# The last output unit of a two-layer decoder trunk: where its residual is added, how its blocks are multiplied, which queue stores

## Chip, cores, metric

One Trainium2 chip, one of its cores. The metric is the device time of one execution in microseconds (us), as the median of several runs. Engines: TensorE (PE, its weight loads PEld), VectorE (DVE), ScalarE (ACT), GpSimd (POOL), SyncE (SP). VectorE, ScalarE and TensorE work on SBUF and on PSUM, where the matmuls accumulate.

## What is computed

Two layers on x of 256 tokens by 2048 features in float32. Layer 0 is forgetting attention (32 heads of 64, logits with a cumulated forget gate), layer 1 is sliding-window attention with sinks and partial rotary. Each has a SiLU gate path, an output projection and a residual; a final RMSNorm closes:

```python
for i in range(DEPTH):
    h = rmsnorm(x, norm_g[i])
    p = h @ w_in                      # q, k, v, gate
    y = attention(q, k, v) * silu(gate)
    x = x + y @ w_out                 # residual
return rmsnorm(x, final_g)
```

The change lies in the last two of these lines of the second layer, for the last 256 of the 2048 features.

## The kernel before

The activations lie with features on partitions: `xT` is 128 partitions x 16 k-tiles x 256 tokens. A float32 product is made of rounded parts: weights and activations are split into a high and a low part (ScalarE casts the high part, line 220, VectorE subtracts for the low one, line 221), and high x high, high x low and low x high are accumulated. The weights come in units of 256 columns. Each has four parts of four k-tiles, which SyncE loads into four raw buffers (line 207); split weights lie in five buffers.

A unit has two blocks, c = 0 and 1 (`block(unit, p, c)`, for part p). Most units (`halves`) multiply wide and narrow: per k-tile one matmul of 512 columns, whose moving operand is the high and the low part side by side, and later one of 256. The high-high and the cross products then lie in two halves of a PSUM bank and are added by VectorE when the unit is consumed. The last unit, `last_out[7]` (`halves=False`, `apart`), has tokens on partitions instead: block c is token half c, it has an accumulator of its own, and the plain branch makes three matmuls of 256 columns per k-tile into one half bank. Accumulators rotate over the two buffers of pool `ps_acc`; a new one waits until the reader of the one before last is done.

The order on TensorE is that of the program text (`keep_in_program_order`). On the other engines a planner orders by priority and readiness. Steps are counted by `tick()`, four for a part's block, so 32 for a unit; `after(n, fn)` issues `fn` n steps later, with raised priority.

The tail. Units 0 to 6 of the last projection add their residual in `xT` on VectorE (lines 697 and 698), square (line 712, summed on GpSimd, line 718) and scale by the norm's weights. `tail_residual`, 20 steps after layer 1's norm, turns the last two k-tiles of `xT` by four TensorE transposes into `tail_x` (tokens on partitions). `columns`, 16 steps after unit 6, makes the sum of squares of units 0 to 6 per token. In the last unit all four parts of c = 0 come first, then those of c = 1. When a block is done, `finish(th, ps)` adds `tail_x` (line 782), sums squares (line 786), makes r = 1/sqrt by Ln and Exp and one Newton step (lines 789 to 797) and multiplies by the last weights (line 798). `scale` then spreads r over partitions by a matmul (`rows`), multiplies the other 14 k-tiles by it in four pieces (`scaled`, line 811) and stores all. For th = 0 `scale` comes `SCALE_DUE` = 8 steps later, that is after two parts of c = 1; for th = 1 at once. Stores alternate between SyncE's and ScalarE's queues.

Of the kernel before, what the change touches and what calls it, by code (L numbers as in the profile page):

```python
# [10 lines left out]
F32 = mybir.dt.float32  # L11
F32R = mybir.dt.float32r
AF = mybir.ActivationFunctionType
ALU = mybir.AluOpType
AX = mybir.AxisListType

P = 128
S = 256
D = 2048
KT = D // P  # L20
# [37 lines left out]
def trunk(  # L58
# [19 lines left out]
    def mm(*args, **kw):  # L78
        tc.keep_in_program_order(nc.tensor.matmul(*args, **kw))  # L79

    def transpose(out, in_, ident):
        tc.keep_in_program_order(nc.tensor.transpose(out, in_, ident))  # L82
# [22 lines left out]
    def after(steps, fn):  # L105
        due.setdefault(clock[0] + max(steps, 1), []).append(fn)
# [117 lines left out]
    def block(unit, p, c):  # L224
        _, _, _, kt0, s = unit.parts[p]
        w, a = loaded[unit, p], unit.acts
        if p == 0 and (c == 0 or unit.apart):

            pool, tag, banks = unit.apart if c == 1 else (*unit.acc, 2)
            ps = pool.tile([P, banks, 512], F32, tag=tag, name="acc")  # L230
            if unit.apart:
                unit.ps[c] = ps[:, 0, :]
            else:
                unit.ps, unit.both = [ps[:, i, :] for i in range(2)], ps
        n = unit.n if unit.kind == "tok" else S
        both, ps = unit.ps[c], unit.ps[c][:, 0:n]
        cs = slice(c * P, (c + 1) * P)
        def operands(i):

            kt = kt0 + i  # L240
            if unit.kind == "tok":
                return a[:, kt, 0, cs], a[:, kt, 1, cs], w[:, i]
            return w[:, i, 0, cs], w[:, i, 1, cs], a[:, kt]

        first, last = kt0 == 0, kt0 + s == KT
        ops = [operands(i) for i in range(s)]
        def done():
            if p < len(unit.parts) - 1:
                return
            if unit.apart:  # L250
                unit.consume(c, both)
            elif c == 1 and unit.kind == "tok":
                for i in range(2):
                    unit.consume(i, unit.ps[i])
            elif c == 1:
                unit.consume(unit.both)

        def narrow():
            for i, (_, sl, mv) in enumerate(ops):
                mm(ps, sl, mv[:, 0, :], start=False, stop=last and i == s - 1)  # L260
                if i % 2:
                    tick()
            done()

        if unit.halves:

            for i, (sh, _, mv) in enumerate(ops):
                mm(both, sh, mv.rearrange("p h n -> p (h n)"), start=first and i == 0, stop=False)
                if i % 2:
                    tick()  # L270
            if s % 2:
                tick()
            return narrow
        if n == 512:
            for i, (sh, sl, mv) in enumerate(ops):
                mm(ps, sh, mv[:, 0, :], start=first and i == 0, stop=False)
                mm(ps, sh, mv[:, 1, :], start=False, stop=False)
                tick()
                mm(ps, sl, mv[:, 0, :], start=False, stop=last and i == s - 1)
                tick()  # L280
        else:
            for i, (sh, sl, mv) in enumerate(ops):
                mm(ps, sh, mv[:, 0, :], start=first and i == 0, stop=False)
                mm(ps, sl, mv[:, 0, :], start=False, stop=False)
            for i, (sh, _, mv) in enumerate(ops):
                mm(ps, sh, mv[:, 1, :], start=False, stop=last and i == s - 1)
                tick()
        done()
        return lambda: None
# [434 lines left out]
    def to_layer1(m):  # L724
        split_x(m, 1)
        square_into(sums1, m)
        if m == KT - 1:

            def norm():
                nonlocal swa  # L730
                fox_scope.__exit__(None, None, None)
                swa = ctx.enter_context(tc.tile_pool(name="swa", bufs=2))
                state["r1"] = r = inv_rms(
                    sums1, "n1", ps_s.tile([P, 2, 512], F32, tag="S", name="ps_n1")[:, 0, :]
                )
                rope = swa.tile([P, 2, S], F32, name="rope_c", bufs=1)
                nc.sync.dma_start(out=rope, in_=rope_d)
                nc.vector.tensor_mul(rope, rope, r[:, 0:S].unsqueeze(1).to_broadcast([P, 2, S]))
                state["rr"] = rope
                after(20, tail_residual)  # L740

            after(19, norm)

# [2 lines left out]
    FM = KT - 2  # L746
    tail = {}

    def tail_residual():
        pt = ps_t.tile([P, 512], F32, tag="T", name="pt_r")  # L750
        for th in range(2):
            for j in range(2):
                o = (2 * th + j) * P
                transpose(pt[:, o : o + P], xT[:, FM + j, th * P : (th + 1) * P], ident)
        tail["x"] = swa.tile([P, 2, 2 * P], F32, name="tail_x", bufs=1)
        nc.scalar.copy(tail["x"], pt.rearrange("p (t f) -> p t f", t=2))

    def to_end(m):
        square_into(sums2, m)
# [18 lines left out]

    def finish(th, ps):
        t = slice(th * P, (th + 1) * P)  # L780
        x = tail["x"][:, th, :]
        nc.vector.tensor_add(x, ps[:, 0 : 2 * P], x)
        rest = work.tile([P, 2, 3 * P], F32, tag="st", name="rest").rearrange("p a b -> p (a b)")
        xg, sq = rest[:, 0:S], rest[:, S : 2 * S]
        ss, v, r, w = (work.tile([P, 1], F32, tag=f"tail{i}", name=f"tail{i}") for i in range(4))
        nc.vector.tensor_tensor_reduce(
            out=sq, in0=x, in1=x, scale=1.0, scalar=0.0, op0=ALU.mult, op1=ALU.add, accum_out=ss
        )
        nc.vector.tensor_scalar(
            v, ss, 1.0 / D, tail["ss"][:, th : th + 1], op0=ALU.mult, op1=ALU.add  # L790
        )
        nc.scalar.activation(r, ss, AF.Ln, scale=1.0 / D, bias=tail["ss"][:, th : th + 1])
        nc.scalar.activation(r, r, AF.Exp, scale=-0.5)

        nc.vector.scalar_tensor_tensor(out=w, in0=r, scalar=-0.5, in1=r, op0=ALU.mult, op1=ALU.mult)
        nc.vector.tensor_scalar(w, w, v, 1.5, op0=ALU.mult, op1=ALU.add)
        nc.vector.tensor_mul(r, r, w)
        nc.vector.tensor_mul(xg, x, tail["g"])

        def scale():  # L800
            rows = ps_s.tile([P, 2, 512], F32, tag="S", name="rows")[:, 0, :]
            mm(rows[:, 0:P], r.to_broadcast([P, P]), ident, start=True, stop=True)
            nc.scalar.mul(xg, xg, r)
            nc.scalar.dma_start(out=tail_d[th], in_=xg)

            scaled = wpool.tile([P, 2048], F32, tag="w", name="scaled")
            scaled = scaled[:, 0 : FM * P].rearrange("p (m t) -> p m t", t=P)
            m0 = 0
            for i, n in enumerate((2, 4, 4, 4)):
                m1 = m0 + n  # L810
                nc.vector.tensor_mul(  # L811
                    scaled[:, m0:m1, :], xT[:, m0:m1, t],
                    rows[:, 0:P].unsqueeze(1).to_broadcast([P, n, P]),
                )
                eng = (nc.sync, nc.scalar)[i % 2]
                eng.dma_start(out=out_d[th, :, m0:m1, :], in_=scaled[:, m0:m1, :])
                m0 = m1

        if th == 0:
            after(SCALE_DUE, scale)  # L820
        else:
            scale()
# [195 lines left out]
    for i, (u, p) in enumerate(stream):  # L1018
        if u in paired:
            if p % 2 == 0:  # L1020
                if prev is not None:
                    block(*prev, 1)()
                    prev = None
                fetch(i + WBUFS)
            held += [block(u, p, c) for c in range(2)]
            if p % 2:
                for k, narrow in enumerate(held):
                    narrow()
                    if k == 1:
                        fetch(i + WBUFS)  # L1030
                held = []
            continue
        fetch(i + 1 + LOOK)
        if u is last_out[7]:
            if p == 0 and prev is not None:
                block(*prev, 1)()
            block(u, p, 0)()
            continue
        block(u, p, 0)()
        if prev is not None:  # L1040
            block(*prev, 1)()
        prev = (u, p)
    for p in range(len(last_out[7].parts)):
        block(last_out[7], p, 1)()


# [63 lines left out]
```

## Time and profile before

| | us |
|---|---|
| median of 3 runs (lowest, highest) | 823.14 (822.63, 824.35) |
| the profiled execution | 824.22 |
| its span, first to last instruction | 822.5 |
| TensorE busy | 812.5 |
| VectorE busy | 633.2 |
| ScalarE busy | 526.5 |
| GpSimd busy | 57.8 |

The span is what the profiler saw between the first and the last instruction; the time of the execution is a little longer. The mean granted TensorE clock was 0.997 of full speed. In the rows below, a timeline row is start, length, engine, line, operation, output and inputs, and how many instructions it merges; in brackets stands how long the engine had been idle before it and what ended that. A row of weight loads (LDWEIGHTS) shows at what moment TensorE takes up each matmul.

### The profile page before, as it was taken

To read this page: it belongs to the slowest core of one execution; us is meant where nothing else is said; L and a number is where in the kernel's file an instruction comes from. 1 tells how busy PE (TensorE), PEld (TensorE's weight loads), DVE (VectorE), ACT (ScalarE), POOL (GpSimd) and SP (SyncE) were. 2 spreads that over 40 slices of the span, in tenths; PEclk is the share of its full clock that TensorE was granted. 3 is DMA by queue.
4 is the path that set the end of the run, shared out by engine and by line. 5 is a ranking of instruction groups with operands and counts; after the bars stand their busy time and mean duration, and the time that the engine had idled before them with its cause. 6 is when DMAs were issued, how large, how long until landed. Compare 5 with 4: busy or idle time off the path is not lost.

```text
span 822.5 us, 13113 instructions
## 1 busy us (share of the span) xinstructions
PE 812.5 (99%) x4738; PEld 707.4 (86%) x4738; DVE 633.2 (77%) x1179; ACT 526.5 (64%) x978; POOL 57.8 (7%) x96
## 2 busy tenths in 40 slices
PE   9999999999999999999999999999999999999996
PEld 8888888888888888888888888888888888887886
DVE  6998866887668776788749668788999899976655
ACT  6875765675666665575737555577678776875642
POOL 1012010100001010020002110000000000001210
PEclk9999999999999999999999999999999999999998
DMA  8766665665656565565555555655455454464642
GB/s 286 234 219 228 192 205 181 192 201 174 190 188 182 190 212 179 181 196 160 178 186 183 191 191 162 200 179 176 130 174 174 156 166 152 154 194 145 205 128 103
DMA packets 47264, 150.49 MB, mean 183 GB/s; under 512 B 5552, under 2 KB 7248, under 8 KB 47200
## 3 DMA queue, kind: packets, MB, share of 16 engines
q1 hardware_dynamic: 44640, 141.71, 54.1%
q0 software_dynamic: 1408, 6.36, 2.8%
q10 hardware_dynamic: 1152, 1.60, 0.5%
q8 instruction: 37, 0.61, 0.3%
q14 instruction: 27, 0.22, 0.1%
HBM read 147.50 MB, written 2.15 MB: 182 GB/s over the span
## 4 chain that ended last, share of the span: by engine, by line
PE 96%; DMA 2%; DVE 1%; SPq 1%; ACT 0%; issue 0%; DVEq 0%; ACTq 0%
PE acc L79 88%; PE ps_s L79 3%; PE psy L79 3%; PE pt L82 1%; DMA wraw<-in_vf_dram 1%; PE pt_w L82 1%; DMA wraw<-in_fox_in_dram 1%; SPq L207 0%; DVE xs L155 0%; DVE scaled L811 0%; DVE w L221 0%; PE ps_n L79 0%; SPq L930 0%; DVE ssq L942 0%; PE rows L79 0%
## 5 line engine op out<-in xcount | busy, mean ns | idle before, releaser
L79 PE MATMUL acc<-xs,w 128*128 128x512 f32 (+1 forms) x2624 | 478.1, 339 | 0.4 <-ACT w L220 0.4
L79 PEld LDWEIGHTS acc<-xs,w 128*128 128x128 f32 x2624 | 405.1, 190 | 54.4 <-issue 1.3
L221 DVE TENSOR_TENSOR w<-wraw,w 128x1024 fp32r<-128x1024 f32 (+4 forms) x277 | 324.7, 1181 | 115.5 <-ACT w L220 113.5
L220 ACT CAST w<-wraw 128x1024 fp32r<-128x1024 f32 (+4 forms) x277 | 276.7, 1009 | 135.6 <-PE acc L79 99.9
L79 PE MATMUL acc<-ys,w 128*128 128x512 f32 (+1 forms) x960 | 169.7, 338 | 0.0
L79 PEld LDWEIGHTS acc<-ys,w 128*128 128x128 f32 x960 | 147.5, 189 | 20.5 <-issue 0.6
L79 PE MATMUL acc<-w,xs 128*128 128x512 f32 (+2 forms) x512 | 110.8, 364 | 0.5 <-ACT w L220 0.5
L79 PEld LDWEIGHTS acc<-w,xs 128*128 128x128 f32 x512 | 86.9, 191 | 14.6 <-ACT w L220 0.8
L335 ACT ACTIVATE st<-st,mx 128x128 f32<-128x128 f32 (+1 forms) x128 | 56.6, 445 | 17.1 <-DVE mx L639 17.1
L293 ACT COPY half<-acc 128x512 f32<-128x512 f32 x56 | 32.8, 585 | 9.5 <-PE acc L79 8.8
L79 PE MATMUL ps_s<-kk,q 128*128 128x256 f32 (+1 forms) x160 | 31.2, 309 | 0.1
L718 POOL TENSOR_TENSOR acc<-acc,sq 128x256 f32<-128x256 f32 x28 | 23.7, 848 | 89.0 <-ACT sq L712 87.9
L390 DVE CUSTOM_DVE_ANT_0 st<-ps_s,st 128x128 f32<-128x128 f32 (+1 forms) x96 | 28.1, 330 | 0.4
L79 PEld LDWEIGHTS ps_s<-kk,q 128*128 128x128 f32 x160 | 24.3, 189 | 3.2 <-issue 0.8
L517 ACT CAST ys<-gt 128x512 fp32r<-128x512 f32 x16 | 9.9, 619 | 22.8 <-DVE gt L516 22.8
L424 ACT COPY pts<-pt 128x384 f32<-128x384 f32 x32 | 15.2, 474 | 14.4 <-PE pt L82 14.1
L335 ACT ACTIVATION_READ_ACCUMULATOR st<-st,mx 128x1 f32 x128 | 24.1, 188 | 0.0
L716 POOL COPY acc<-sq 128x256 f32<-128x256 f32 x2 | 1.3, 674 | 323.5 <-ACT sq L712 323.5
L626 POOL DMA_DIRECT2D bc<-negc_d x16 | 8.8, 552 | 216.8 <-DVE st L415 144.0
L310 ACT ACTIVATE gate_e<-gt 128x512 f32<-128x512 f32 x16 | 10.1, 628 | 21.3 <-DVE gt L323 21.3
L123 POOL TENSOR_SCALAR_AFFINE_SELECT bc<-bc 128x256 f32<-128x256 f32 x32 | 18.7, 605 | 71.0 <-DMA bc<-negc_d 71.0
L154 ACT ACTIVATE xs<-xT,g_sb 128x256 fp32r<-128x256 f32 x32 | 15.5, 501 | 12.8 <-DVE xT L698 12.0
(144 smaller groups left out, 596.9 us busy)
## 6 DMA issues: line engine op xcount, KB each, us to landing
wraw<-in_fox_in_dram SPq DMA_DIRECT2D x96, 512.0 KB, 4.5
wraw<-in_swa_in_dram SPq DMA_DIRECT2D x72, 512.0 KB, 3.9
wraw<-in_fox_out_dram SPq DMA_DIRECT2D x32, 512.0 KB, 3.9
wraw<-in_swa_out_dram SPq DMA_DIRECT2D x32, 512.0 KB, 4.1
wraw<-in_fox_in_dram SPq DMA_DIRECT2D x54, 256.0 KB, 4.2
bc<-negc_d POOLq DMA_DIRECT2D x16, 384.0 KB, 5.3
wraw<-in_vf_dram SPq DMA_DIRECT2D x4, 288.0 KB, 5.2
xT<-in_xt_dram SPq DMA_DIRECT2D x2, 512.0 KB, 9.2
```

The costliest lines, as they stand in the source:

```text
L79: tc.keep_in_program_order(nc.tensor.matmul(*args, **kw))
L82: tc.keep_in_program_order(nc.tensor.transpose(out, in_, ident))
L123: return nc.gpsimd.affine_select(out=ap, in_=ap, compare_op=ALU.is_ge, fill=NEG, base=base, pattern=pattern, channel_multiplier=mult,)
L154: nc.scalar.activation(xs[:, kt, 0, :], xT[:, kt, :], AF.Copy, scale=g)
L220: state["split"] = nc.scalar.copy(high, raw)
L221: nc.vector.tensor_tensor(out=low, in0=raw, in1=high.bitcast(F32), op=ALU.subtract)
L293: nc.scalar.copy(s, ps[:, :, S : 2 * S])
L310: nc.scalar.activation(e, z, AF.Abs)
L335: nc.scalar.activation(st[:, hh, rng], st[:, hh, rng], AF.Exp, bias=nm[:, qb, hh : hh + 1], accum_out=l[:, qb, hh : hh + 1],)
L390: nc.vector.tensor_tensor_reduce(out=st, in0=high, in1=st, scale=self.scale, scalar=LOWEST, op0=ALU.add, op1=ALU.max, accum_out=self.mx[:, ...
L424: nc.scalar.copy(group.new_pts(self.j, hh)[:, hh, self.j, :], pt[:, 0 : 3 * P])
L718: nc.gpsimd.tensor_add(sums[0], sums[0], s)
```

## The change

Four edits, all for the last unit.

1. `tail_residual` no longer uses TensorE, PSUM and ScalarE. VectorE turns `xT`'s last two k-tiles in blocks of 32 x 32, one GpSimd DMA writes the result to a DRAM tile, and 16 GpSimd DMAs (128 rows of 32 elements each) read it back in the right order into `tail_x`. It is timed 150 steps after the step that was followed by 20.
2. Block c = 0 of the last unit takes the wide and narrow branch. Its `finish` adds both halves of the bank, so it has one VectorE add more.
3. The first part of block c = 1 moves up to just behind the second part of c = 0. Then VectorE adds the residual of th = 1 to that accumulator in PSUM, and the other three parts accumulate on top, after c = 0 is done. `finish(1)` reads PSUM directly: no add, and the squares are summed by ScalarE instead of VectorE.
4. All stores of th = 0 go through SyncE's queue; those of th = 1 still alternate.

```diff
-        if unit.halves:
+        if unit.halves or (unit.apart and unit.kind == "tok" and unit.n == 256 and c == 0):
...
         else:
+            seeds = bool(unit.apart) and n == 256
+            kw = {"skip_group_check": True} if seeds else {}
...
-                mm(ps, sh, mv[:, 1, :], start=False, stop=last and i == s - 1)
+                mm(ps, sh, mv[:, 1, :], start=False, stop=(last or seeds) and i == s - 1, **kw)
...
-                after(20, tail_residual)
+                after(150, tail_residual)
...
+    turned_d = dram.tile([P, 2, 4, 64], F32, name="turned_d")
+
     def tail_residual():
-        pt = ps_t.tile([P, 512], F32, tag="T", name="pt_r")
-        for th in range(2):
-            for j in range(2):
-                o = (2 * th + j) * P
-                transpose(pt[:, o : o + P], xT[:, FM + j, th * P : (th + 1) * P], ident)
-        tail["x"] = swa.tile([P, 2, 2 * P], F32, name="tail_x", bufs=1)
-        nc.scalar.copy(tail["x"], pt.rearrange("p (t f) -> p t f", t=2))
+        turned = swa.tile([P, 2, 4, 64], F32, name="turned", bufs=1)
+        nc.vector.transpose(
+            turned.rearrange("p t b (k j) -> p k (t b) j", k=2),
+            xT[:, FM:KT, :].rearrange("p k (b j) -> p k b j", j=32),
+        )
+        nc.gpsimd.dma_start(out=turned_d, in_=turned)
+        x = tail["x"] = swa.tile([P, 2, 2 * P], F32, name="tail_x", bufs=1)
+        rows = turned_d.rearrange("(a i) t b (k j) -> a t b i k j", a=4, k=2)
+        cols = x.rearrange("p t (k a j) -> a t p k j", k=2, a=4)
+        for t in range(2):
+            for a in range(4):
+                for k in range(2):
+                    nc.gpsimd.dma_start(out=cols[a, t, :, k], in_=rows[a, t, :, :, k])
...
     def finish(th, ps):
-        x = tail["x"][:, th, :]
-        nc.vector.tensor_add(x, ps[:, 0 : 2 * P], x)
+        if th == 0:
+            x = tail["x"][:, th, :]
+            nc.vector.tensor_add(x, ps[:, 0:S], x)
+            nc.vector.tensor_add(x, ps[:, S : 2 * S], x)
+        else:
+            x = ps[:, 0:S]
...
-        nc.vector.tensor_tensor_reduce(
-            out=sq, in0=x, in1=x, scale=1.0, scalar=0.0, op0=ALU.mult, op1=ALU.add, accum_out=ss
-        )
+        if th == 0:
+            nc.vector.tensor_tensor_reduce(
+                out=sq, in0=x, in1=x, scale=1.0, scalar=0.0, op0=ALU.mult, op1=ALU.add, accum_out=ss
+            )
+        else:
+            nc.scalar.activation(sq, x, AF.Square, accum_out=ss)
...
-            nc.scalar.dma_start(out=tail_d[th], in_=xg)
+            (nc.sync, nc.scalar)[th].dma_start(out=tail_d[th], in_=xg)
...
-                eng = (nc.sync, nc.scalar)[i % 2]
+                eng = (nc.sync, nc.scalar)[i % 2 * th]
...
             block(u, p, 0)()
+            if p == 1:
+                block(u, 0, 1)()
+                seeded = u.ps[1][:, 0:S]
+                nc.vector.tensor_add(seeded, seeded, tail["x"][:, 1, :])
             continue
...
-    for p in range(len(last_out[7].parts)):
+    for p in range(1, len(last_out[7].parts)):
         block(last_out[7], p, 1)()
```

More of the change, by code (lines that the diff above doesn't have):

```diff
@@ L281, in block @@
         else:
+            seeds = bool(unit.apart) and n == 256
+            kw = {"skip_group_check": True} if seeds else {}
             for i, (sh, sl, mv) in enumerate(ops):
-                mm(ps, sh, mv[:, 0, :], start=first and i == 0, stop=False)
-                mm(ps, sl, mv[:, 0, :], start=False, stop=False)
+                mm(ps, sh, mv[:, 0, :], start=first and i == 0, stop=False, **kw)
+                mm(ps, sl, mv[:, 0, :], start=False, stop=False, **kw)
             for i, (sh, _, mv) in enumerate(ops):
-                mm(ps, sh, mv[:, 1, :], start=False, stop=last and i == s - 1)
+                mm(ps, sh, mv[:, 1, :], start=False, stop=(last or seeds) and i == s - 1, **kw)
                 tick()
```

## The prediction

> **What bounds the kernel now.** I read the page's busy rows first, then the whole chain of waits with TensorE's own waits, and last the timeline of the final 20 us, where most of the change sits.
>
> ```profile
> PE 812.5 (99%) x4738; PEld 707.4 (86%) x4738; DVE 633.2 (77%) x1179; ACT 526.5 (64%) x978; POOL 57.8 (7%) x96
> ...
> PE 96%; DMA 2%; DVE 1%; SPq 1%; ACT 0%; issue 0%; DVEq 0%; ACTq 0%
> ...
> PE rows L79 <- DVE tail L797: 2.3, 1, 2.3
> ```
>
> TensorE is busy for 99% of the span, carries 96% of the chain, and the longest it ever waits for another engine is 2.3 us, once, in the last unit's tail (the columns of a wait: us in all, times, longest). So time comes off in two ways only: less work on TensorE anywhere, or a shorter stretch behind its last matmul. That stretch, from the chain that ended last:
>
> ```profile
> 814.32 0.43 DVE tail_x L782
> ...
> 814.78 0.42 DVE rest L786
> ...
> 815.25 0.30 ACT tail L792
> ...
> 815.81 0.17 DVE tail L795
> ...
> 816.25 0.17 DVE tail L797
> ...
> 816.56 0.47 PE rows L79 x2
> ...
> 818.07 1.20 DVE scaled L811 x2
> ```
>
> I call E the moment the add L782 starts (814.32). From E the root r is ready after 2.10 us (816.42), its three small steps beginning at E+1.49 (815.81); rows and scaled end at 819.27, and the span ends 3.2 us later, when the stores have landed. The profiled execution took 824.22 us around a span of 822.5; the median of the runs is 823.14, 1.08 lower. I sum against 824.22 and move the difference onto the median.
>
> **The change part by part.** *The transposes off TensorE.* Here are the weight-load rows around the four removed transposes, and those around like groups of four (start, length of the group, instructions). A ScalarE copy goes with them; TensorE doesn't wait for it, so it counts as 0.
>
> ```profile
> 506.32 0.59 PEld L82 LDWEIGHTS pt_r<-ident,xT 128*128 128x128 f32 x4
> 506.87 6.10 PEld L79 LDWEIGHTS acc<-w,xs 128*128 128x128 f32 x35
> ...
> 549.70 0.46 PEld L82 LDWEIGHTS pt_w<-ident,st 128*128 128x128 f32 x4
> 550.13 5.64 PEld L79 LDWEIGHTS acc<-xs,w 128*128 128x128 f32 x32
> 555.71 0.46 PEld L82 LDWEIGHTS pt_w<-ident,st 128*128 128x128 f32 x4
> ```
>
> From the first load to the next unit's load the four took 0.55 us; the like group took 0.43 (549.70 to 550.13). TensorE has no slack there, so all of it comes off: 0.43, between 0.35 (an estimate: 0.43 less the spread of 0.1 between these two) and 0.55.
>
> In its place VectorE turns 512 elements per partition. That form isn't in the trace; the nearest row is the shuffle of the same shape. GpSimd gets 17 DMA issues. In the rows of two stretches of 12 us below, the columns behind the stretch's length are PE, PEld, DVE, ACT and POOL busy.
>
> ```profile
> L838 DVE STREAM_SHUFFLE rot<-rot_t 128x512 f32<-128x512 f32 x9 | 6.7, 743 | 0.0
> ...
> 534.00:546.00 12.00, 12.00 (x75) 10.76 (x74) 8.77 (x22) 7.00 (x17) 0.00 (x0) 1.00 0.55 176
> 546.00:558.00 12.00, 12.00 (x74) 10.70 (x73) 11.93 (x30) 11.01 (x28) 0.00 (x0) 1.00 0.57 175
> ...
> L737 SPq DMA_DIRECT2D rope_c<-in_rope_dram x1: 328/328/328, 419.4 to 419.4; - x1
> ...
> L626 POOL DMA_DIRECT2D bc<-negc_d x16 | 8.8, 552 | 216.8 <-DVE st L415 144.0 <-DVE mx L390 46.6 <-issue 22.0
> ```
>
> 150 steps are 130 later than now. A unit is 32 steps, so 506.4 moves four units on, to about 554, where VectorE is busy 11.93 of 12 us. If the 0.74 us stands ahead of the fold that pt_w at 555.71 reads, TensorE could wait up to 0.74. I take 0: only TensorE keeps program order, and an operation without a late input is moved forward freely (rope's load, written in the same norm step as the residual's timer, went out at 419.4), so the idle 3 us in 534 to 546 are as likely a place. GpSimd's 17 issues are 17 x 0.55 = 9.4 us on an engine at 0.00 there; nobody reads tail_x before about 806. Zero, but see the second rival.
>
> *First block wide and narrow.* Per k-tile three 256-column matmuls become one of 512 and one of 256. The rows of the last unit:
>
> ```profile
> 801.83 5.83 PEld L79 LDWEIGHTS acc<-w,ys 128*128 128x128 f32 x48
> ...
> 804.21 0.69 DVE L698 TENSOR_TENSOR xT<-acc,xT 128x512 f32<-128x512 f32 x1
> ...
> 805.49 1.55 POOL L718 TENSOR_TENSOR acc<-acc,sq 128x256 f32<-128x256 f32 x2 [8.65 <-ACT sq L712]
> ...
> 807.59 0.54 PEld L79 LDWEIGHTS ps_cols<-ones,acc 128*128 128x128 f32 x4
> 807.91 0.42 DVE L782 TENSOR_TENSOR tail_x<-acc,tail_x 128x256 f32<-128x256 f32 x1 [3.02 <-PE acc L79]
> ...
> 808.05 2.94 PEld L79 LDWEIGHTS acc<-w,ys 128*128 128x128 f32 x24
> ...
> 809.85 0.16 DVE L797 TENSOR_TENSOR tail<-tail,tail 128x1 f32<-128x1 f32 x1
> ...
> 810.91 0.31 PEld L79 LDWEIGHTS rows<-ident,tail 128*128 128x128 f32 x2
> 811.14 2.94 PEld L79 LDWEIGHTS acc<-w,ys 128*128 128x128 f32 x24
> 811.45 2.21 DVE L811 TENSOR_TENSOR scaled<-xT,rows 128x256 f32<-128x256 f32 x4 [1.44 <-PE rows L79]
> ```
>
> 48 in 5.76 us and 24 in 2.86 make 0.1197 us each, 0.359 per k-tile. A wide and a narrow one cost (555.71 - 550.13)/16 = 0.349. Sixteen k-tiles: -0.17. Not under zero gain, since the columns are the same; at most 0.33 (0.020 a k-tile, if the second block's pace is the slower 2.94/24). The second add for th = 0 has a price on VectorE, below.
>
> *A new wait.* The second block's first part now comes after two parts of the first. There are two accumulators: the first block takes one, the second must take unit 6's, which VectorE gives back when L698 ends, at 804.90. Two parts of 4 x 0.349 bring TensorE to 801.83 + 2.79 = 804.62, its matmul to 804.74 (0.12 behind the load); with 0.14 from VectorE's end to TensorE's start (816.42 to 816.56) it starts at 805.04. So +0.30, in a place where TensorE doesn't wait today (the block began at 808.05); from 0 to 0.4. Everything on TensorE queues behind it. The seed add waits for those 12 matmuls and has nothing behind it on VectorE until the columns.
>
> From there: second block part 0 (1.44) to 806.36, part 2 (1.40) to 807.75, columns (0.46) to 808.21, whose sum GpSimd has at 807.04, part 3 to 809.61, then 24 matmuls (2.87) to 812.48 for rows. Is r of th = 0 there? Add at 809.61 + 0.32, then 2.10 as today (807.91 to 810.01) and 0.46 for the second add: 812.49, load 0.11 later at 812.60. So +0.12 (0 to 0.25): the cover of 0.9 us that r had today is used up by the added VectorE step and the faster first block. Rows 0.23, last 12 matmuls 1.44, to 814.27, where today it is 814.01: E moves +0.26 (-0.17 + 0.30 + 0.12, rounded), without the transposes.
>
> *The end of th = 1.* The add goes (the residual is in PSUM) and the square goes to ScalarE. Its price, from an activation with a sum:
>
> ```profile
> 545.05 0.49 ACT L335 ACTIVATE st<-st,mx 128x256 f32<-128x256 f32 x1
> 545.46 0.19 ACT L335 ACTIVATION_READ_ACCUMULATOR st<-st,mx 128x1 f32 x1
> ...
> L473 ACT COPY pts<-pt_w x16: 350/362/380, 550.5 to 737.8; 128x256 f32<-128x256 f32 x16
> L475 DVE TENSOR_TENSOR pts<-pt_w,apart x16: 658/684/692, 551.3 to 738.2; 128x512 f32<-128x512 f32 x16
> ```
>
> 0.60 us, then 0.56 through Ln and Exp (815.25 to 815.81): the small steps could begin at E+1.18 instead of E+1.49. But VectorE isn't free: rows of th = 0 used to have 24 matmuls behind them, now 12. Its four scaled products run from 812.60 + 0.54 to 815.35, which is E+0.77 with E at 814.58. Then the product with tail_g (0.34) and v (0.20): E+1.31. I take -0.18, at best -0.31.
>
> *Stores.* Five of th = 0 on SyncE at 0.34 each; its last leaves near 815.7. ScalarE's queue is free for the Square. Cost 0 to 0.2, if they still drain when th = 1's begin near 817.5; I take 0, from their 2.1 us to landing:
>
> ```profile
> out_dram<-scaled SPq DMA_DIRECT2D x2, 256.0 KB, 2.1
> ```
>
> Sum: -0.43 - 0.17 + 0.30 + 0.12 - 0.18 = -0.36 us: 823.9 against 824.22, and 822.8 against the median. All ends together: -0.55 - 0.33 + 0 + 0 - 0.31 = -1.2, and -0.35 + 0 + 0.4 + 0.25 + 0.1 + 0.2 + 0.74 = +1.3 (the 0.1 if the tail loses slightly, the 0.74 the turn).
>
> **The rivals.** *The product first.* L473 and L475 read one PSUM tile from two engines; the last copy starts at 737.8, takes 0.36, and the product starts at 738.2: not together. If the product with tail_g is put ahead of the Square, it runs from E+0.77 to E+1.19, the Square after it, and the small steps begin at E+2.37, 0.88 later than today: sum +0.70, 823.8. The code writes the Square first, which speaks against it. The Trainium skill ("PSUM — Partial Sum Buffer", section "PSUM bank collisions raise a hardware error") says that two engines may not touch one bank in the same partitions at once, reads included; the trace agrees in the two rows named. Were it not so, the two could overlap and their order would cost nothing.
>
> *Slower: the gather holds up weights.* 16 transfers of 128 rows of 128 bytes pass the same 16 DMA engines as the weights.
>
> ```profile
> q0 software_dynamic: 1408, 6.36, 2.8%
> ...
> q10 hardware_dynamic: 1152, 1.60, 0.5%
> ...
> wraw<-in_swa_in_dram SPq DMA_DIRECT2D x72, 512.0 KB, 3.9
> ...
> 553.85 0.33 SPq L207 DMA_DIRECT2D wraw<-in_swa_in_dram  x1
> ...
> 562.50 1.05 ACT L220 CAST w<-wraw 128x1024 fp32r<-128x1024 f32 x1
> ```
>
> q10's packet costs 0.5% x 822.5 x 16 / 1152 = 57 ns, q0's 262 ns (they are larger). 128 packets an engine are 7.3 to 34 us. With four raw buffers, the load issued at 553.85 is cast four casts on, at 562.50: 8.65 us less 3.9 to land leaves 4.75. Loads sharing the engines half and half take 7.8: hidden. It decides once a load is held over 4.75 us: all 7.3 us ahead of one load would cost 2.5, sum +2.2: 825.3. GpSimd's pace of 0.55 us an issue speaks against such a heap. The Trainium skill's page "DMA: Bandwidth & Descriptors" (section "Measured") calls transfers under 64 KB descriptor-dominated, 0.68 us at 4 KB and 0.95 at 64; sixteen of 16 KB would be, as an estimate, 11 to 15 us on end, which no run here shows yet.
>
> *Everything fits:* no accumulator wait, no wait for r, the best prices: 821.9.
>
> **How the numbers follow.** The sum as forecast 0.62; the product first 0.1; slower by the gather 0.08; everything fits 0.2. Two tenths of a per cent are 1.65 us, about what a measurement of this kernel can tell from no change. Forecast and product-first lie within it, a wait behind the turn too; the everything-fits case is 0.4 us short of the bound at 821.5, and the runs scatter by more than that (822.63 to 824.35), so I let 0.12 of its 0.2 pass it. Faster 0.12, within 0.80, slower 0.08. Predicted 822.8, range 821.4 to 824.3: the low end is everything-fits with 0.5 of spread, the high end the sum's upper end (824.4).
>
> **What would show it.** The pt_r rows gone from TensorE; one TensorE wait on L698 of 0.2 to 0.4 us near 804.6; E between 814.0 and 814.3; rows of th = 0 within 0.2 us of r; the Square at E, its small steps at E+1.3 behind scaled; no new ScalarE waits on wraw while GpSimd issues. A wait of TensorE anywhere in 500 to 600, or stores that still land more than 3.4 us after the last scaled product, would make it wrong.

## The result, and the profile after

| us | before | after |
|---|---|---|
| median of 8 runs (lowest, highest) | 823.22 (822.63, 824.35) | 825.34 (824.97, 827.04) |
| the profiled execution, its span | 824.22, 822.5 | 825.25, 823.5 |
| layer 1's first weight load (U) to the last unit's first load | 310.20 | 311.20 |
| from there to the end of the last scaled product | 17.44 | 17.51 |
| from there to the end of the span | 3.23 | 4.04 |

The ratio of the times is 1.0025, with an interval of 1.0016 to 1.0034: the change costs 2.1 us, and the forecast had the wrong sign. What lies ahead of U varies from one execution to the next (U is 491.63 in the profile before, 490.75 after, and the code ahead of it is the same), so the three stages are counted from U; they add up to +1.88. The end of the span is shown to a tenth of a us, so the third stage is good to 0.05 us, and a difference of two such to 0.1. Stages of equal code agree well: the first was 310.20, 310.21 and 310.21 in the three kernels in which nothing ahead of the last unit differs. Only the last unit, which I had worked out most closely, came out as forecast.

The rows of the page and of its waits that answer to those of before:

```profile
span 823.5 us, 13100 instructions
...
PE 812.2 (99%) x4718; PEld 706.8 (86%) x4718; DVE 634.4 (77%) x1179; ACT 526.3 (64%) x979; POOL 67.9 (8%) x113
...
PEld ps_n L79 <- POOL acc L720: 1.6, 1, 1.6
PE rows L79 <- DVE tail L815: 2.1, 1, 2.1
```

TensorE has 20 instructions fewer and is busy 0.3 us less, GpSimd 10 us more. The wait of the tail has shrunk from 2.3 to 2.1, and a wait that was not there before has come: TensorE on GpSimd, 1.6 us, in layer 1's norm (`ps_n` is the matmul that spreads the sum of squares). This is the place, by the timeline of before and then of after:

```profile
491.63 6.80 PEld L79 LDWEIGHTS acc<-xs,w 128*128 128x128 f32 x38
496.56 1.62 POOL L718 TENSOR_TENSOR acc<-acc,sq 128x256 f32<-128x256 f32 x2 [9.52 <-ACT sq L712]
498.17 2.36 DVE L221 TENSOR_TENSOR w<-wraw,w 128x1024 fp32r<-128x1024 f32 x2 [0.59 <-ACT w L220]
498.48 0.42 PEld L79 LDWEIGHTS ps_n<-acc,ones 128*128 128x128 f32 x2
```

```profile
490.75 6.80 PEld L79 LDWEIGHTS acc<-xs,w 128*128 128x128 f32 x38
494.78 0.71 DVE L756 STREAM_TRANSPOSE turned<-xT 128x512 f32<-128x512 f32 x1
496.05 0.57 POOL L760 DMA_DIRECT2D turned_d<-turned  x1 [9.89 <-DVE xs L155]
496.64 0.76 POOL L720 TENSOR_TENSOR acc<-acc,sq 128x256 f32<-128x256 f32 x1
497.28 1.22 DVE L221 TENSOR_TENSOR w<-wraw,w 128x1024 fp32r<-128x1024 f32 x1 [0.77 <-ACT w L220]
497.48 1.61 POOL L720 TENSOR_TENSOR acc<-acc,sq 128x256 f32<-128x256 f32 x1
498.43 1.74 DVE L221 TENSOR_TENSOR w<-wraw,w 128x1024 fp32r<-128x1024 f32 x1
499.14 0.30 PEld L79 LDWEIGHTS ps_n<-acc,ones 128*128 128x128 f32 x2 [1.59 <-POOL acc L720]
500.07 5.41 POOL L767 DMA_DIRECT2D tail_x<-turned_d  x8 [0.98 <-DMA turned_d<-turned]
```

Read it from U. The turn is written for a moment 150 steps after the norm, but it went out at U+4.03, *inside* the norm, and its write to DRAM was put ahead of the last two sums of squares in GpSimd's queue. Before, the sums began at U+4.93 and ended at U+6.55, just when VectorE began to split the next weights (U+6.54). After, the write takes that place: GpSimd first stands idle for it until U+5.30, 0.56 us behind the end of the turn, and then issues for 0.57. The first sum begins at U+5.89, 0.96 later than before, and the second now starts behind the beginning of VectorE's split (U+6.53 as before). It takes 1.61 us instead of 0.80 and ends 0.59 us after the split (498.50, 499.09); the next split, issued before the sum ends, takes 1.74 instead of 1.22. So 0.96 of queue became 1.79 (U+8.34 against U+6.55), and TensorE, which had reached `ps_n` with 0.3 us to spare, waits 1.59.

The last unit after:

```profile
801.95 2.88 PEld L79 LDWEIGHTS acc<-w,ys 128*128 128x128 f32 x16
804.31 0.69 DVE L700 TENSOR_TENSOR xT<-acc,xT 128x512 f32<-128x512 f32 x1
805.12 2.90 PEld L79 LDWEIGHTS acc<-w,ys 128*128 128x128 f32 x20 [0.30 <-issue]
...
812.49 0.16 DVE L815 TENSOR_TENSOR tail<-tail,tail 128x1 f32<-128x1 f32 x1
812.77 0.30 PEld L79 LDWEIGHTS rows<-ident,tail 128*128 128x128 f32 x2
813.29 2.21 DVE L829 TENSOR_TENSOR scaled<-xT,rows 128x256 f32<-128x256 f32 x4 [0.64 <-PE rows L79]
814.73 0.38 ACT L806 ACTIVATE rest<-acc 128x256 f32<-128x256 f32 x1 [1.53 <-PE acc L79]
815.80 0.16 DVE L813 SCALAR_TENSOR_TENSOR tail<-tail 128x1 f32<-128x1 f32 x1 [0.16 <-ACT tail L811]
815.87 0.42 DVE L816 TENSOR_TENSOR rest<-acc,tail_g 128x256 f32<-128x256 f32 x1
816.45 0.16 DVE L815 TENSOR_TENSOR tail<-tail,tail 128x1 f32<-128x1 f32 x1
817.25 2.21 DVE L829 TENSOR_TENSOR scaled<-xT,rows 128x256 f32<-128x256 f32 x4 [0.64 <-PE rows L79]
```

The accumulator wait is the 0.30 in brackets. E, the start of the Square, is 12.78 us after the unit's first load (before 12.49), and r is ready at E+1.88 (before E+2.10).

The end of the program, by the rows of its closing instructions, before and then after (count, then shortest/median/longest in ns, then first to last start):

```profile
L1104 SPq DRAIN  x2: 7/7/7, 821.7 to 821.8; - x2
L1104 POOLq EVENT_SEMAPHORE  x2: 17/17/17, 822.3 to 822.4; - x2
```

```profile
L1126 SPq EVENT_SEMAPHORE  x1: 28/28/28, 821.9 to 821.9; - x1
L1126 SPq DRAIN  x1: 7/7/7, 821.9 to 821.9; - x1
L1126 SPq DRAIN  x1: 116/116/116, 822.3 to 822.3; - x1
L1126 POOLq EVENT_SEMAPHORE  x1: 17/17/17, 823.0 to 823.0; - x1
L1126 POOLq EVENT_SEMAPHORE  x1: 17/17/17, 823.4 to 823.4; - x1
```

SyncE's two drains stood 0.1 us apart and now stand 0.4 apart; GpSimd's two last semaphores stood 0.1 apart and now 0.4. No wait is listed in these gaps, and the stores land 1.7 to 2.2 us after their issue in both kernels, the last of them 2.2 us behind the last scaled product (821.5 before, 821.7 after). What follows, 1.0 us before and 1.8 after, is closing instructions. The gaps are some 0.6 of the 0.8 by which the ending is longer.

### The profile page after: what moved, and what is told of

It is laid out like the page before. It is cut to its first block, busy times and chain, and to the rows that moved or that the text cites. A ratio compares the mean times of both kernels' runs of the same rounds, so it can differ in the third digit from the quotient of the medians.

```text
span 823.5 us, 13100 instructions
## 1 busy us (share of the span) xinstructions
PE 812.2 (99%) x4718; PEld 706.8 (86%) x4718; DVE 634.4 (77%) x1179; ACT 526.3 (64%) x979; POOL 67.9 (8%) x113
## 4 chain that ended last, share of the span: by engine, by line
PE 97%; DVE 1%; DMA 0%; POOL 0%; ACT 0%; issue 0%; DVEq 0%; SPq 0%
PE acc L79 89%; PE ps_s L79 3%; PE psy L79 3%; PE pt L82 1%; PE pt_w L82 1%; DMA wraw<-in_vf_dram 0%; POOL acc L720 0%; DVE w L221 0%; DVE scaled L829 0%; ACT w L220 0%; PE ps_n L79 0%; PE rows L79 0%; DVE turned L756 0%; DVE xT L699 0%; DVE xT L700 0%
## 5 line engine op out<-in xcount | busy, mean ns | idle before, releaser
L123 POOL TENSOR_SCALAR_AFFINE_SELECT bc<-bc 128x256 f32<-128x256 f32 x32 | 16.6, 538 | 68.7 <-DMA bc<-negc_d 68.7
```

Source lines behind the costliest of these rows:

```text
L123: return nc.gpsimd.affine_select(out=ap, in_=ap, compare_op=ALU.is_ge, fill=NEG, base=base, pattern=pattern, channel_multiplier=mult,)
```

## The experiments

Three questions, each with a theory and a rival. *The norm's wait*: is it the order in GpSimd's queue, or the turn on VectorE and its traffic at that place? *The ending*: is it the late stores on SyncE's queue, or something that has to do with the queues' programs? *The last unit*: are its terms those of the forecast? Below, a kernel's three stages are written as in the table (before 310.20, 17.44, 3.23; after 311.20, 17.51, 4.04), and the ratio is against the kernel before, measured beside it.

**The turn alone** (the kernel before with edit 1 only)

```diff
-                after(20, tail_residual)
+                after(150, tail_residual)
     ... and the new tail_residual
```

> The kernel before with the first edit alone (the turn by VectorE and through DRAM). Theory A, the GpSimd queue: the write of the turned block is moved ahead of the last two sums of squares of layer 1, TensorE waits about 1.6 us for them at the norm, less 0.5 for the four transposes gone: 1.1 us slower than before, the wait of ps_n on GpSimd in the trace. If the longer end of the span (0.8 us) also comes from GpSimd's 17 DMA issues, 1.9 slower (825.1). Rival B, the last unit is what costs: this kernel is 0.4 us faster than before (822.8).

824.84 us against 823.47, ratio 1.0017 [1.0008, 1.0025]. Stages 311.20, 17.44, 3.57. The wait is there in full:

```profile
498.19 0.30 PEld L79 LDWEIGHTS ps_n<-acc,ones 128*128 128x128 f32 x2 [1.59 <-POOL acc L718]
```

Edit 1 by itself loses 1.0 in the first stage, as much as all four edits, and some 0.3 at the end, which no store of edit 4 can explain.

**Everything but the turn** (the changed kernel with the four transposes on TensorE)

```diff
-                after(150, tail_residual)
+                after(20, tail_residual)
     ... and the old tail_residual
```

> The changed kernel with the old turn by TensorE, 20 steps after the norm; the other three edits stay. Theory A: no wait at the norm, 1.1 us less than the changed kernel (824.2), and if the longer end comes from GpSimd's issues 1.9 less (823.4, about 0.1 above before). Rival B: no less than 825.3, since the last unit's edits are all in.

823.77 against 823.47, 0.9999 [0.999, 1.0008]. Stages 310.21, 17.51, 3.68: the norm is as before, the last unit as after, and +0.45 remains of the ending. The two endings add up as far as can be told: 0.34 + 0.45 = 0.79, measured 0.81.

**The write behind the sums.** The turn stays where the planner puts it; only its write must follow the last sum on GpSimd.

```diff
-            nc.gpsimd.tensor_add(sums[0], sums[0], s)
+            state["summed"] = nc.gpsimd.tensor_add(sums[0], sums[0], s)
...
-        nc.gpsimd.dma_start(out=turned_d, in_=turned)
+        with tc.issue_after(state["summed"].ins):
+            nc.gpsimd.dma_start(out=turned_d, in_=turned)
```

> The changed kernel with one order fixed: GpSimd issues the write of the turned block behind the last sum of squares of layer 1. Theory A: the wait of 1.6 us at the norm goes, 823.7. A rival within A, that VectorE's turn (0.71 us) delays the splits and squares and so the norm: the wait stays at 0.7 us or more, 824.5 or more. Rival B: 825.3.

823.81 against 823.47, 1.0003 [0.9995, 1.0012]; stages 309.75, 17.51, 3.98. Its timeline:

```profile
494.79 0.71 DVE L756 STREAM_TRANSPOSE turned<-xT 128x512 f32<-128x512 f32 x1
495.69 1.67 POOL L720 TENSOR_TENSOR acc<-acc,sq 128x256 f32<-128x256 f32 x2 [9.51 <-ACT sq L714]
497.30 0.57 POOL L761 DMA_DIRECT2D turned_d<-turned  x1
497.61 0.42 PEld L79 LDWEIGHTS ps_n<-acc,ones 128*128 128x128 f32 x2
```

The turn starts within 0.01 us of its old time, and the wait is gone. So it was the order in the queue, neither VectorE's time nor the gather. Without the wait the turn is worth what it was meant to be: 309.75 against 310.20, -0.45.

**The turn late.** VectorE's turn is bound behind the low split of its own step.

```diff
-        nc.vector.tensor_tensor(out=low, ...)
+        state["low"] = nc.vector.tensor_tensor(out=low, ...)
...
+        with tc.issue_after(state["low"].ins):
             nc.vector.transpose(...)
```

> The changed kernel with VectorE's turn held where its step stands in the program, near 554 us, where VectorE is busy 11.9 of 12 us, instead of 495 us. If the turn costs nothing there: no wait at the norm, the time of e3 (823.8). If it delays the fold that pt_w reads, a wait of TensorE of up to 0.7 us near 556 and up to 824.5.

823.54 against 823.50, 1.0004 [0.9995, 1.0013]; stages 309.75, 17.50, 3.98. The turn now lies where the timer had meant it to be:

```profile
553.03 0.68 DVE L757 STREAM_TRANSPOSE turned<-xT 128x512 f32<-128x512 f32 x1
554.50 0.46 PEld L82 LDWEIGHTS pt_w<-ident,st 128*128 128x128 f32 x4
```

It is in the busy stretch for which I had kept 0.74 us as an upper bound, and `pt_w` doesn't wait. The first stage is that of the kernel above.

**Two writes instead of one**, to double the suspected cost.

```diff
-        nc.gpsimd.dma_start(out=turned_d, in_=turned)
+        for t in range(2):
+            nc.gpsimd.dma_start(out=turned_d[:, t], in_=turned[:, t])
```

> The changed kernel with the write of the turned block cut into two GpSimd DMAs (one for each token half); they are issued one ahead of each of the last two sums. Theory A, time on GpSimd's queue: another 0.55 to 0.6 us of issue ahead of the norm, TensorE waits 2.1 to 2.3 us for the sum instead of 1.6. Rival, that the wait is for the turn or for the squares: 1.6 us again.

One run: 825.68 against 823.49, with no interval. Stages 311.21, 17.51, 4.07: the wait did not grow, which I had expected of it.

```profile
496.51 0.57 POOL L761 DMA_DIRECT2D turned_d<-turned  x1 [9.89 <-DVE xs L155]
497.10 0.75 POOL L720 TENSOR_TENSOR acc<-acc,sq 128x256 f32<-128x256 f32 x1
497.75 1.23 DVE L221 TENSOR_TENSOR w<-wraw,w 128x1024 fp32r<-128x1024 f32 x1 [0.77 <-ACT w L220]
497.79 0.56 POOL L761 DMA_DIRECT2D turned_d<-turned  x1
498.36 1.19 POOL L720 TENSOR_TENSOR acc<-acc,sq 128x256 f32<-128x256 f32 x1
...
PEld ps_n L79 <- POOL acc L720: 1.6, 1, 1.6
```

The order became write, sum, write, sum, and the second write lies beside the split, in time which the second sum had spent stretched. U is 491.21 here, so that the sums end at U+8.34, to the hundredth as with one write. A DMA issue runs beside VectorE's split at full pace; the sum ends 0.57 to 0.59 us after that split, whether it is issued 0.61 or 0.20 us into it. So the size of the wait is set by when VectorE's split ends, and the write matters because it pushes a sum behind the split's start.

The Trainium skill ("SBUF — State Buffer", section "Who interferes with whom") says that a VectorE instruction with two inputs in SBUF contends with a GpSimd instruction that reads SBUF, calls the shared port pair an exclusive lock, and says that issue order decides who blocks. The rows agree: the split issued first held the sum, and the sum held the next split (1.74 for 1.22).

**The stores alternating again** (the changed kernel without edit 4)

```diff
-            (nc.sync, nc.scalar)[th].dma_start(out=tail_d[th], in_=xg)
+            nc.scalar.dma_start(out=tail_d[th], in_=xg)
...
-                eng = (nc.sync, nc.scalar)[i % 2 * th]
+                eng = (nc.sync, nc.scalar)[i % 2]
```

> The changed kernel with the stores of th = 0 alternating again as before. If five stores on SyncE made the end of the span longer, from the last scaled product to the end takes 3.2 us as before instead of 4.0, and the time is 824.5; ScalarE's Square may start up to 0.35 us late behind a store. If not, 825.3 and 4.0 us.

824.91 against 823.47, 1.0019 [1.001, 1.0027]; stages 311.20, 17.67, 3.52. The ending gains some 0.5, but the last unit loses 0.16, for a store of ScalarE's now stands between the two small activations of the tail (chain that ended last):

```profile
815.21 0.29 ACT tail L810
815.50 0.34 ACTq L834
815.89 0.21 ACT tail L811
```

**Edit 4 alone** on the kernel before

```diff
-            nc.scalar.dma_start(out=tail_d[th], in_=xg)
+            (nc.sync, nc.scalar)[th].dma_start(out=tail_d[th], in_=xg)
...
-                eng = (nc.sync, nc.scalar)[i % 2]
+                eng = (nc.sync, nc.scalar)[i % 2 * th]
```

> The kernel before with the fourth edit alone, all stores of th = 0 on SyncE. If these stores by themselves make the end longer: from the last scaled product to the end 3.7 us instead of 3.2, 0.45 slower than before (823.9). If the longer end needs the other edits: 3.2 us, and no change (823.4).

824.07 against 823.50, 1.0008 [0.9999, 1.0017]; stages 310.21, 17.68, 3.78. The ending is some 0.5 longer; the interval of the ratio just holds one, so this rests on the profile. The last unit's 0.24 is in `rows` of th = 1, which took 0.72 us instead of 0.47; the same is in the mixed kernel below, and why, stays open.

**The moved part one part later, and the stores mixed.** First the write behind the sums as above, and the seeded part behind three parts of c = 0 instead of two:

```diff
-            if p == 1:
+            if p == 2:
                 block(u, 0, 1)()
```

> As e3 (write behind the sums), and the first part of the second block comes behind the third part of the first instead of the second. Theory: TensorE's 0.30 us wait for unit 6's accumulator goes, nothing else moves: 0.3 less than e3, 823.5 where the kernel before is at 823.4. Rival: the wait only covers for one that comes later (r of th = 0 or the seed), and the time stays that of e3.

823.29 against 823.50, 1.0 [0.9991, 1.0009]; stages 309.75, 17.17, 4.05. The accumulator wait is gone and with it 0.34 us. Then, on top, ScalarE's queue for two of the stores of th = 0:

```diff
+            nc.scalar.dma_start(out=tail_d[th], in_=xg)
...
+                eng = (nc.sync, nc.scalar)[i % 2 if th or i < 2 else 0]
```

> As e5, and of the stores of th = 0 the last block and the second piece go to ScalarE, three go to SyncE (two in the kernel before, five in the changed one). Theory: SyncE's gap of 0.35 us between its last semaphore and its drain goes, from the last scaled product to the end takes 3.5 us instead of 4.0: 0.45 less than e5, 823.1, at or a little under the kernel before. Rival, that the gap comes from the th = 1 end itself: no change against e5.

822.91 against 823.50, 0.9995 [0.9986, 1.0004]; stages 309.75, 17.27, 3.67. I had expected SyncE's gap to go with two stores fewer on it. It has not gone: it now stands before SyncE's last drain, where it holds up the end by some 0.1 us only; GpSimd's is left.

```profile
L1127 SPq EVENT_SEMAPHORE  x1: 17/17/17, 820.9 to 820.9; - x1
L1127 SPq DRAIN  x1: 130/130/130, 821.2 to 821.2; - x1
```

**What the gaps are.** They came with edit 4 on SyncE and with edit 1 on GpSimd, 300 us before the end. Theory: a queue's program has grown by a few instructions, and some boundary falls into the closing instructions. Rival: the stores and gathers themselves. First, the kernel before with three more loads on SyncE, of a few bytes that nothing reads; they went out at 417.9 to 418.9, 400 us from the end:

```diff
+                extra = swa.tile([P, 32], F32, name="extra", bufs=1)
+                for i in range(3):
+                    after(24 + 16 * i, lambda i=i: nc.sync.dma_start(out=extra[0:H, i : i + 1], in_=bf_d))
```

> The kernel before with three small extra loads on SyncE in the middle of the run (32 rows of 4 bytes, read by nobody), stores as before. Theory L, the length of SyncE's program decides where it stalls at the end: a gap of 0.35 us appears among SyncE's last instructions as in the changed kernel, and the span's end comes 0.4 to 0.5 us later behind the last scaled product (3.7 instead of 3.2). Rival S, the stores themselves: 3.2, no gap.

824.39 against 823.49, 1.0011 [1.0002, 1.002]; stages 310.36, 17.43, 4.02.

```profile
L1107 SPq DRAIN  x1: 7/7/7, 820.4 to 820.4; - x1
L1107 SPq DRAIN  x1: 130/130/130, 820.7 to 820.7; - x1
```

Three idle loads, with the stores as they were, bring the gap of SyncE. The ending is longer than the 3.7 I expected for another reason. Before, SyncE's closing waits for the stores come in three steps, of 0.8 us at most; here SyncE waits once, 2.3 us, for the store that lands last, and takes its other semaphores one by one behind it. Its first drain so stands 2.79 us behind the last product instead of 2.43.

Next, the kernel with the later part and 24 idle GpSimd writes of one column at the program's start, which move GpSimd's program on:

```diff
+    for _ in range(24):
+        nc.gpsimd.memset(pad, 0.0)
```

> As e5, with 24 small memsets more on GpSimd early in the run (2 to 3 us of an idle engine). Theory L: GpSimd's gap of 0.35 us before its last instruction moves out of the ending, from the last scaled product to the end 3.7 instead of 4.05, 0.35 less time than e5. Rival S, that the 17 DMAs of the turn must be closed at the end: 4.05 as in e5, or more.

822.63 against 823.49, 0.9991 [0.9982, 1.0]; stages 309.77, 17.17, 3.74: more work on GpSimd, and its gap is gone (4.05 without). The two semaphores stand together again:

```profile
L1130 POOLq EVENT_SEMAPHORE  x2: 17/17/17, 820.4 to 820.5; - x2
```

Last, both queues padded, SyncE by 24 of the idle loads above:

```diff
-                for i in range(3):
+                for i in range(24):
```

> As e11, with 24 small extra loads on SyncE too, between the weight loads of layer 0's projection. Theory L: both gaps are out of the ending, 3.2 to 3.3 us from the last scaled product to the end, 0.75 less than e5: 822.6 where the kernel before is at 823.4, the first version that is clearly faster. Rival: the extra loads hold up weights, a wait of TensorE on ScalarE's casts between 419 and 490.

822.60 against 823.49, 0.999 [0.9981, 0.9999]; stages 309.93, 17.16, 3.25.

```profile
L1133 SPq DRAIN  x2: 7/7/7, 820.0 to 820.3; - x2
L1133 POOLq EVENT_SEMAPHORE  x2: 17/17/17, 820.6 to 820.7; - x2
```

SyncE has three drains at the end, and the row of two holds the second and the third: they stand 2.45, 2.50 and 2.75 us behind the last product, where the kernel before has 2.43, 2.48 and 2.73. The ending is back at that of before, with all stores of th = 0 on SyncE and the whole gather on GpSimd.

Counting instructions in the traces says where the gaps are. SyncE's gap stands in front of the 592nd instruction that the trace lists for it, in each of the ten kernels that reach that number in their ending; GpSimd's stands in front of its 197th, in each of eight. Every gap is 0.34 to 0.37 us long. With two writes GpSimd has one instruction more, and the gap comes one step earlier among its closing ones. The kernel before ends with SyncE's 591st and GpSimd's 178th, and the kernel with both queues padded passes the two places 34 and 62 us before its end. So a gap belongs to a place in a queue's program and not to what its instructions do.

What an engine does in a gap is not seen. Behind each of the 18 gaps the traces have a packet of 8 KB on q14, a queue that the page lists as `instruction`: 0.6 to 0.7 us behind the gap's end, once 0.9. The Trainium skill ("Runtime: NRT & Kernel Launch", section "Instruction fetch mechanics") says that an engine's instructions are fetched in blocks of 256 and that crossing one is mostly hidden. The fixed places and the packets fit a crossing in the closing instructions that is not hidden, some 0.35 us each; that this is what the gap is, is an inference.

This last kernel is 0.9 us under the kernel before, with an interval that just leaves one out; the changed one was 2.1 above its own. Its time can't be told from that of the kernel above (822.63): its ending is 0.5 shorter, but its U is 0.5 later and its first stage 0.16 longer. It keeps all four edits, two of them placed differently (the write of edit 1, the moved part of edit 3).

## Why the prediction was wrong

The sum forecast -0.36 us; the stages gave +1.88. (The top of the range stands as 824.3, where its sum gives 824.4.) By its terms:

- *Transposes off TensorE, -0.43*: right in size (-0.45 with the write behind the sums), lost through the term that follows.
- *The turn by VectorE and GpSimd's 17 issues, 0*: the step that failed. I wrote that GpSimd is "at 0.00 there" and that "nobody reads tail_x before about 806". Both are true of the place around 554 and of the gather, and neither asks what the first of the 17 is put in front of. In the same paragraph I argued that the planner moves such an operation forward freely, by rope's load at 419.4, and then costed the early place on VectorE alone (the 0.74 that never came due). GpSimd at the early place had a row in the timeline, the two sums of the norm that end as TensorE takes them up; one issue of 0.57 ahead of them, with GpSimd's wait for the turn before it, cost +1.45 (311.20 against 309.75). Each issue of the gather took 0.68 rather than 0.55, which cost nothing.
- *Wide and narrow -0.17, accumulator wait +0.30, wait for r +0.12, tail -0.18, together +0.07*: measured +0.07, and each term came. Counted from load to load, the first block took 5.58 us without the wait (2.80, 1.40 and 1.38) against 5.76. The wait is 0.30 in its row and 0.37 from the moment when the next load was due (804.75); the later place of the moved part gained 0.34. The wait for r is 0.11: loads follow each other every 0.12 us, the last of the 24 was taken up at 812.54, and `rows` only at 812.77, 0.12 behind r. E moved by 0.29 (forecast 0.26), and r came at E+1.88 (forecast E+1.92). VectorE was through with scaled at E+0.77, as forecast. The small steps began at E+1.07 and not at E+1.31, for the product with tail_g, 0.34 us, slipped in behind the first of them instead of ahead, and so took back most of the gain.
- *Stores, 0 (0 to 0.2)*: the second step that failed. I read the 3.2 us behind the last product as the time until the stores have landed, and as fixed but for that landing. They have landed after 2.2 us, before and after; the closing instructions of SyncE and GpSimd behind it cost 0.8 more, some 0.45 with edit 4 and some 0.3 with edit 1, a cost outside every term I had listed.
- *Rivals.* "The product first" did not come: the Square was first, and the product never ran beside it. "The gather holds up weights" was the right sign with the wrong mechanism: no cast waits longer for its raw weights, since GpSimd strings the sixteen issues out from 500 to 511. I had counted 128 packets an engine for the gather; by the page q0 grew from 1408 packets to 2000, write included, which is 37 an engine. Of the two signs that I had named as proof against me, the wait of TensorE came a microsecond ahead of its window of 500 to 600 (499.14), and the stores did not land late: the ending of 4.04 us comes from the closing instructions behind them.

## What to carry to other kernels

An operation that a planner may move forward has to be costed at the earliest place its inputs allow, on each in-order queue that it uses, against whatever it could be put in front of there; a queue that is 93% idle can still be the last to arrive at one point. If a timer is meant as a place, bind the operation behind an instruction. And at differences of a microsecond look at the closing instructions as well, for a few instructions more on a queue, anywhere in the program, moved the end by a third of a microsecond.

## What the runs showed of the hardware

- A GpSimd add of 128x256 float32 that meets VectorE's 128x1024 subtraction is held to 0.6 us after that one's end (1.61 us instead of 0.80), and holds the next in turn (1.74 instead of 1.22). A GpSimd DMA issue beside the same subtraction kept its 0.56 us.
- The ending depends on the length of a queue's program, through gaps of 0.34 to 0.37 us at fixed places (ahead of the 592nd instruction listed for SyncE and the 197th for GpSimd): 3.23 us in the kernel before, 4.05 in the changed kernel with its part moved later, 3.74 and 3.25 when GpSimd's and then also SyncE's program was made longer still.
- VectorE turned 128x512 float32 in 32 x 32 blocks in 0.68 to 0.71 us.
